# Two edits to a hand-made scheduler: due times without the delay inside an engine, and transfers planned to land later

## The chip, the cores and the metric

The kernel runs on 1 core of one Trainium2 chip. The metric is device time in microseconds from the first to the last work of one execution. Inputs and weights start in the chip's memory, all in float32, and the output goes back there.

## The reference

One layer of a hybrid encoder on 256 tokens of width 2048, with 256 fixed memory tokens:

```python
x = x + 0.5 * swiglu(rms_norm(x, ffn1_norm), ffn1_w_up, ffn1_w_down)      # d_ff 5632
h = rms_norm(x, mix_norm)
q_a, f_a, i_a, g_a, x_b, gate_b, gates = split(h @ w_in)
y_a = rms_norm(hgrn2(q_a, f_a, i_a)) * silu(g_a)          # gated linear recurrence, 8 heads
y_b = rglru(causal_conv4(x_b)) * gelu(gate_b)             # linear scan over the tokens
g = sigmoid(gates + b_gate)
x = x + (g[0] * (y_a @ w_branch_a) + g[1] * (y_b @ w_branch_b)) @ w_out
x = x + cross_attention(rms_norm(x), rms_norm(mem))       # 4 heads, wq, wkv, wo
x = x + 0.5 * swiglu(rms_norm(x, ffn2_norm), ffn2_w_up, ffn2_w_down)
return rms_norm(x, final_norm)
```

All weights together are several hundred MB and are read once.

## The kernel before

**The arithmetic.** Every large product is made of float32 parts that TensorE takes in one pass (`float32r`). A weight tile of 128 x 2048 (1 MB) is loaded into `raw`; ScalarE (ACT) writes its rounded high part `h`, VectorE (DVE) the rest `l = raw - h` (function `split`). The activations are split likewise. A product is then h·high + h·low + l·high, so each weight tile costs one ScalarE pass, one VectorE pass and three sets of matmuls.

**The stages.** In order: `ffn1`, the input projection ("in", "v", "gate") with the two recurrent branches in between, "ab" and "out", cross-attention ("q", "k", "mv", "o"), and `ffn2`. Three forms of product matter:

- `product` (stages "in", "q", "k"; 72 weight tiles): one bank of PSUM (the accumulators; there are eight) collects 16 matmuls of 512 columns with `h` as the stationary operand, and 16 of 256 columns with `l`. In the trace they are `acc<-ops,h` and `acc<-ops,l`.
- `rows_product` (stages "v", "gate", "ab", "out", "mv", "o"): two banks, the weights are the moving operand, all matmuls have 512 columns. In the trace `acc<-h,ops` and `acc<-l,ops`.
- `ffn`: the up projection combines two by two blocks with seven products instead of eight ("fast"); that needs sums of weight blocks (`td`, split into `th` and `tl`). Each of 11 blocks of hidden features ends with a chain on VectorE and ScalarE over the tile `ev`, transposes on TensorE, and the split operand `hidop`. The down projection ("down", 12 matmuls into each of two banks per weight tile) follows a few pieces later.

Two further ways to make a weight's parts: "added" (in `ffn1`) loads `own` on SP's queue, ScalarE writes `l = -round(own)`, and a DMA on POOL's queue adds `own` to it while it lands. "made" (for `ffn2`) computes block sums ahead of time, in the stages between the feed-forwards, and keeps them in the chip's memory: `made` is loaded, VectorE takes differences, and `kept` is stored by POOL's queue, to be read as `td` later.

**The order.** Nothing runs as it is written. `Flow.record` keeps each operation with the operations it depends on; `arrange` then plays the program through with modelled costs and writes one fixed sequence for all engines, which `emit` issues. The engines keep that sequence in hardware, each in its own order, waiting for each other on semaphores. What the planner uses:

- `price`: the modelled duration `op.busy` of each operation, and for a DMA the time `op.moved` that its bytes take in a shared pipe (2.9 us per MB, 5.2 us if it accumulates).
- `nominal`: the time at which a TensorE operation would start if TensorE ran the program as written without a hole.
- `aims`: from the last operation back, each operation's due time `op.due`. TensorE's operations start from their `nominal`; every operation is then due early enough for each of its successors, that is at `s.due - lag`. Successors include the next user of a buffer.
- `LAG`: per engine, the delay from the end of an operation to the start of its reader. `op.spent` is `op.busy` plus this delay, plus, for a DMA, `moved + LANDS`.
- In the play, each engine takes the ready operation with the lowest due time among those whose `nominal` is not more than `AHEAD` past the point reached. TensorE's true float32 operations (transposes and small products, marked `turn`) are gathered: within `STICK` of the first one due they may go ahead. A DMA waits while the pipe is filled for more than `BACKLOG`, its end is `dma + LANDS`, and the 9 to 13 big buffers are handed out by due time (`Ring.fit`).
- Between two operations of one engine the play already counts no `LAG` (it has `r = t + busy`, with 0.1 more on VectorE and ScalarE where the second reads the first's output); `aims` does.

The sequence is computed twice; the second time the due times follow the first sequence and its use of buffers.

Of the kernel before, what the change touches and what calls it, by code (L numbers as in the profile page):

```python
# [176 lines left out]


LAG = {"PE": 0.24, "DVE": 0.15, "ACT": 0.16, "POOL": 0.16, "SP": 0.1}
AHEAD, BACKLOG, STICK, LANDS = 30, 3, 8, 3.5  # L180
TABLES = {ACT.Silu, ACT.Sigmoid, ACT.Sqrt, ACT.Exp, ACT.Gelu_apprx_tanh}


class Flow:
# [97 lines left out]
    def aims(self, order):  # L282
        for op in self.ops:
            op.due = op.nominal if op.queue.name == "PE" or not op.after else 1e9
        for op in reversed(order):
            for s in op.after:
                lag = op.spent if s.deps.get(op, True) is not None else 0
                op.due = min(op.due, s.due - lag)

    def arrange(self):  # L290
# [1369 lines left out]
```

## Time and profile before

| | |
|---|---|
| median of 3 runs | 2427.21 us (2426.22 to 2428.08) |
| the profiled execution's own time | 2425.98 us |
| its span, first to last instruction | 2424.2 us |
| mean granted clock of TensorE | 0.999 |
| TensorE busy | 2408.9 us, 99% of the span, 12130 matmuls |
| VectorE busy | 2066.3 us, 85% |
| ScalarE busy | 1420.8 us, 59% |
| moved by DMA | 662.84 MB, mean 273 GB/s |

A profile is of one execution. "Busy" leaves out waiting, and the weight loads of TensorE (PEld) overlap its matmuls. Nearly all rows carry line 464, the one place where recorded operations are issued, so groups are told apart by their tiles: `acc<-ops,h` means that the bank `acc` was written from operand tiles `ops` and `h`. A duration of a matmul includes its way through the array: the distance between two starts, not the duration, is what one costs in a row of them.

### The profile page before, as it was taken

Reading aid. Unit: us, or ns where it says so; the run is one execution under the profiler, and the core shown is the slowest. Engines: PE = TensorE matmul, PEld = TensorE weight load, DVE = VectorE, ACT = ScalarE, POOL = GpSimd, SP = SyncE. Lnnn points to the kernel's source line nnn. Section 1 sums busy time; section 2 is a strip of 40 time slices with the busy share of each in tenths; the row PEclk is TensorE's granted clock in tenths of the full one; section 3 lists DMA queues with packets and bytes.
Section 4 is the critical chain, followed back from the end, with each engine's and each line's share of the span. In section 5 each row is a group of like instructions: output and inputs, shape, how many; then the busy total and the mean of one; then the engine's idle time right before and its main releaser. Section 6 shows DMA issues by size and latency. Waiting matters only on the chain. (4 is left out here: it accounts for less than half of the span.)

```text
span 2424.2 us, 30937 instructions
## 1 busy us (share of the span) xinstructions
PE 2408.9 (99%) x12130; PEld 2008.3 (83%) x12130; DVE 2066.3 (85%) x2232; ACT 1420.8 (59%) x1411; POOL 83.0 (3%) x142
## 2 busy tenths in 40 slices
PE   9999999999999999999999999999999999999998
PEld 8888888888888888888888888888888788888887
DVE  8999999999955778788876877867899999999995
ACT  8566666666654444467434644445676666666663
POOL 0000000000000000000000000000000000000000
PEclk9999999999999999999999999999999999999999
DMA  8568877877835677888989888886898777777773
GB/s 316 191 226 260 260 255 249 254 248 253 283 125 194 245 289 288 331 304 314 360 293 335 337 320 309 317 293 246 328 383 322 257 256 259 261 259 259 260 285 113
DMA packets 98355, 662.84 MB, mean 273 GB/s; under 512 B 10912, under 2 KB 11168, under 8 KB 24992
## 3 DMA queue, kind: packets, MB, share of 16 engines
q1 hardware_dynamic: 77904, 517.11, 57.5%
q0 software_dynamic: 19584, 142.62, 18.2%
q8 instruction: 95, 1.56, 0.2%
q10 hardware_dynamic: 720, 1.13, 0.1%
q14 instruction: 52, 0.43, 0.0%
HBM read 574.83 MB, written 60.82 MB: 262 GB/s over the span
## 5 line engine op out<-in xcount | busy, mean ns | idle before, releaser
L464 DVE TENSOR_TENSOR l<-raw,h 128x2048 fp32r<-128x2048 f32 (+2 forms) x428 | 870.9, 2039 | 163.6 <-PE acc L464 65.4
L464 ACT ACTIVATE h<-raw 128x2048 fp32r<-128x2048 f32 (+2 forms) x428 | 730.7, 1713 | 449.0 <-DVE l L464 182.0
L464 PE MATMUL acc<-h,xh 128*128 128x512 f32 x1244 | 471.1, 390 | 0.8 <-ACT h L464 0.3
L464 PE MATMUL acc<-h,xl 128*128 128x512 f32 x1244 | 449.3, 389 | 0.0
L464 PE MATMUL acc<-h,hidop 128*128 128x512 f32 x1408 | 440.0, 390 | 0.0
L464 ACT ACTIVATE h<-td 128x1024 fp32r<-128x1024 f32 (+1 forms) x248 | 308.1, 1251 | 199.7 <-DVE td L464 180.8
L464 PE MATMUL acc<-h,ops 128*128 128x512 f32 x1664 | 411.8, 391 | 0.0
L464 PE MATMUL acc<-ops,h 128*128 128x512 f32 x1152 | 391.8, 397 | 0.1
L464 DVE TENSOR_TENSOR tl<-td,h 128x1024 fp32r<-128x1024 f32 (+1 forms) x248 | 360.8, 1463 | 2.4 <-ACT h L464 0.7
L464 PEld LDWEIGHTS acc<-h,ops 128*128 128x128 f32 x1664 | 310.1, 188 | 63.7
L464 PEld LDWEIGHTS acc<-h,hidop 128*128 128x128 f32 x1408 | 262.9, 188 | 53.5
L464 PEld LDWEIGHTS acc<-h,xh 128*128 128x128 f32 x1244 | 233.1, 188 | 51.4 <-ACT h L464 2.0
L464 PEld LDWEIGHTS acc<-h,xl 128*128 128x128 f32 x1244 | 233.5, 188 | 48.3
L464 PE MATMUL acc<-ops,l 128*128 128x256 f32 x1152 | 273.5, 281 | 0.0
L464 PE MATMUL acc<-l,hidop 128*128 128x512 f32 x704 | 264.3, 390 | 2.0 <-DMA l<-own 1.9
L464 PEld LDWEIGHTS acc<-ops,h 128*128 128x128 f32 x1152 | 202.4, 188 | 32.9 <-DVE ops L464 0.9
L464 PEld LDWEIGHTS acc<-ops,l 128*128 128x128 f32 x1152 | 212.6, 188 | 19.8
L464 PE MATMUL acc<-l,ops 128*128 128x512 f32 x832 | 223.0, 390 | 0.0
L464 PE MATMUL acc<-tl,xh 128*128 128x512 f32 x608 | 187.6, 390 | 0.0
L464 PE MATMUL acc<-l,xh 128*128 128x512 f32 x636 | 186.2, 390 | 0.2 <-DVE l L464 0.2
L464 PEld LDWEIGHTS acc<-l,ops 128*128 128x128 f32 x832 | 155.5, 188 | 32.4 <-DVE l L464 0.4
L464 DVE TENSOR_TENSOR made<-made 128x512 f32<-128x512 f32 x224 | 153.4, 688 | 20.3 <-DMA made<-wu 16.7
(172 smaller groups left out, 1918.1 us busy)
## 6 DMA issues: line engine op xcount, KB each, us to landing
raw<-wu SPq DMA_DIRECT2D x108, 1024.0 KB, 7.7
raw<-wd SPq DMA_DIRECT2D x72, 1024.0 KB, 7.5
made<-wu POOLq DMA_DIRECT2D x56, 1024.0 KB, 6.5
kept<-made POOLq DMA_DIRECT2D x56, 1024.0 KB, 6.8
td<-kept SPq DMA_DIRECT2D x56, 1024.0 KB, 6.8
raw<-wu SPq DMA_DIRECT2D x56, 768.0 KB, 5.4
raw<-win SPq DMA_DIRECT2D x40, 1024.0 KB, 5.1
raw<-wg SPq DMA_DIRECT2D x32, 1024.0 KB, 6.5
```

What stands on the lines that cost most here:

```text
L464: getattr(op.queue.real, method)(*map(real, args), **{k: real(v) for k, v in kw.items()})
```

## The change

Two edits in the planner, none in the recorded operations.

In `aims`, the step from an operation to its successor is now the modelled duration alone where both are on the same engine and the first is no DMA; in all other cases with a dependence of order or data it is `op.spent` as before, and 0 where only the hand-out of the buffer is meant.

`LANDS`, the time after a transfer's turn in the pipe at which it is taken to have landed, goes from 3.5 to 4. It enters `op.spent`, so the due times, and the end of each transfer in the play.

```diff
-AHEAD, BACKLOG, STICK, LANDS = 30, 3, 8, 3.5
+AHEAD, BACKLOG, STICK, LANDS = 30, 3, 8, 4
...
             for s in op.after:
-                lag = op.spent if s.deps.get(op, True) is not None else 0
+                behind = s.queue is op.queue and not op.moved
+                lag = 0 if s.deps.get(op, True) is None else op.busy if behind else op.spent
                 op.due = min(op.due, s.due - lag)
```

## The prediction

> **What bounds the kernel now.** I read the page first, then busy time by stretches, TensorE's waits, and last the order of TensorE's matmuls in the stages that the two edits touch.
>
> ```profile
> span 2424.2 us, 30937 instructions
> PE 2408.9 (99%) x12130; PEld 2008.3 (83%) x12130; DVE 2066.3 (85%) x2232; ACT 1420.8 (59%) x1411; POOL 83.0 (3%) x142
> ```
>
> TensorE is busy for 2408.9 of 2424.2 us. 15.3 us are idle, so a better order can win little by filling holes, and a worse one has no upper bound. The profiled execution took 2425.98 us, 1.8 us more than its span and 1.23 us under the median of the runs, 2427.21. I make the sum as a difference and apply it to the median. About 0.2%, 4.85 us, is what a measurement of this kernel can tell from no change.
>
> Busy time by stretches, PE first and VectorE (DVE) third:
>
> ```profile
> 300.00:600.00 300.00, 297.95 (x1330) 245.68 (x1329) 280.87 (x287) 203.47 (x165) 13.01 (x15) 1.00 0.79 248
> 1500.00:1646.00 146.00, 144.93 (x720) 121.69 (x718) 106.09 (x139) 71.38 (x91) 9.62 (x18) 1.00 0.85 305
> 1900.00:2100.00 200.00, 199.76 (x892) 164.89 (x891) 197.90 (x171) 126.22 (x97) 0.00 (x0) 1.00 0.72 262
> 2300.00:2424.00 124.00, 115.22 (x517) 95.28 (x515) 92.78 (x88) 62.98 (x63) 0.00 (x0) 0.98 0.54 200
> ```
>
> 8.8 of the 15.3 us lie in the last stretch, mostly the closing norm and store after the last matmul. 2.05 us lie in 300 to 600, 1.07 in 1500 to 1646. In both feed-forward blocks VectorE is nearly full too: 280.87 of 300 and 197.90 of 200 us. TensorE's own waits:
>
> ```profile
> PE acc L464 <- DMA l<-own: 1.9, 3, 1.0
> PE acc L464 <- DVE p L464: 1.1, 2, 0.6
> PE warm L464 <- DVE ones L464: 1.1, 1, 1.1
> PE acc L464 <- DVE merge L464: 0.5, 1, 0.5
> PE acc L464 <- DVE sum L464: 0.4, 1, 0.4
> PE acc L464 <- ACT h L464: 0.3, 1, 0.3
> ```
>
> The largest is a transfer: the accumulating DMA that makes the low part `l` from `own` in the first feed-forward. The granted clock is 1.00 in all stretches but the last, so it plays no part.
>
> **The change, first edit: dues without the delay.** No instruction is added or removed; only `due`, the key by which the planner picks, moves. Of two operations of one engine the first was due the second's due minus its duration *and* the engine's `LAG`. Now it is the duration alone. TensorE's matmuls into one bank depend on each other, so each link of such a chain brought the earlier one forward by 0.24 us. In `product` (the column products of "in", "q" and "k") 32 matmuls in a row share a bank: 16 with `h` (512 columns), 16 with `l` (256). The first was due 31 x 0.24 = 7.4 us before its place in the program, the last at its place. As a product lasts some 5.6 us, the next product's `h` matmuls sort between the present one's `l` matmuls. The timeline shows just this mixing at its end, and then the last product alone; below it a row product, which has no long chain:
>
> ```profile
> 1535.46 0.40 PE L464 MATMUL acc<-ops,h 128*128 128x512 f32 x1
> 1535.69 0.28 PE L464 MATMUL acc<-ops,l 128*128 128x256 f32 x1
> 1535.81 0.39 PE L464 MATMUL acc<-ops,h 128*128 128x512 f32 x1
> ...
> 1536.50 2.08 PE L464 MATMUL acc<-ops,l 128*128 128x256 f32 x16
> 1538.42 0.40 PE L464 MATMUL acc<-h,ops 128*128 128x512 f32 x1
> ...
> 991.54 3.79 PE L464 MATMUL acc<-h,ops 128*128 128x512 f32 x16
> 995.17 1.98 PE L464 MATMUL acc<-l,ops 128*128 128x512 f32 x8
> ```
>
> Without the 0.24 every link's due equals its program place, and TensorE runs 16 `h`, then 16 `l`, product after product. That matters for the spacing. Alone, 16 `l` matmuls take from 1536.50 to 1538.42, 0.120 us each; 16 matmuls of 512 columns in a row take 991.54 to 995.17, 0.227 each. So a straight pair costs 0.347 us. Mixed, groups by form in two stretches with no other work (65 us, 1465 to 1530, then 60 us, 1380 to 1440) count:
>
> ```profile
> L464 PE MATMUL acc<-ops,h 128*128 128x512 f32 x185 | 61.9, 396 | 0.0
> L464 PE MATMUL acc<-ops,l 128*128 128x256 f32 x187 | 45.3, 281 | 0.0
> ...
> L464 PE MATMUL acc<-ops,h 128*128 128x512 f32 x172 | 57.5, 396 | 0.0
> L464 PE MATMUL acc<-ops,l 128*128 128x256 f32 x171 | 41.5, 281 | 0.0
> ```
>
> Straight, the first would take 185 x 0.227 + 187 x 0.120 = 64.4 of its 65 us, the second 59.6 of 60. That is 0.56 us saved on 185 pairs and 0.44 on 172. The page gives the whole count, and the same 6 ns in the means:
>
> ```profile
> L464 PE MATMUL acc<-h,ops 128*128 128x512 f32 x1664 | 411.8, 391 | 0.0
> L464 PE MATMUL acc<-ops,h 128*128 128x512 f32 x1152 | 391.8, 397 | 0.1
> ```
>
> 1152 pairs (72 products of 16, none missing) save 1152/185 x 0.56 = 3.5 or 1152/172 x 0.44 = 2.9 us; I take **-3.3 us**. TensorE is the path there, so it comes through whole. The ends: 0, if 0.233 belongs to these operands and not to the mixing; -6.9, if each mixed `h` loses 6 ns and the short `l` ones give nothing back.
>
> [...]
>
> In `down`, 12 matmuls share a bank and `h` ran up to 11 x 0.24 = 2.6 us early. All have 512 columns there, so straight order changes no spacing. It asks for `h` 2.6 us later, which loosens the loads. At the very end, token half 0's last matmul now has 12 behind it; before, 11:
>
> ```profile
> 2412.34 0.39 PE L464 MATMUL acc<-l,hidop 128*128 128x512 f32 x1
> 2412.56 1.75 PE L464 MATMUL acc<-h,hidop 128*128 128x512 f32 x7
> 2414.15 1.07 PE L464 MATMUL acc<-l,hidop 128*128 128x512 f32 x4
> ```
>
> So half 0's closing chain starts one matmul, **0.2 us**, earlier, and half 1's residual add, which comes after it on VectorE, has that much less ahead of it. Bounds: 0, if half 1's last matmul alone sets the end, and 0.23.
>
> VectorE's chains (sums of banks, `td`, `made`) become due 0.15 us later per link. They fall behind splits more often; the cover is the four pieces of 21 matmuls between a block's sums and its transposes, 4 x 21 x 0.227 = 19 us. I cost that at 0; its loss is the third rival.
>
> **The second edit: LANDS 4.** A 1 MB load is planned to land 2.9 + 0.06 + 4 = 6.96 us after its issue instead of 6.46; one that accumulates, 5.2 + 0.9 + 4 = 10.1 instead of 9.6. Each DMA on SP's and POOL's queues becomes due 0.5 us earlier, `own` and its accumulation together 1.0, and its readers are placed 0.5 us later. The trace's landings:
>
> ```profile
> raw<-wu SPq DMA_DIRECT2D x108, 1024.0 KB, 7.7
> td<-kept SPq DMA_DIRECT2D x56, 1024.0 KB, 6.8
> raw<-win SPq DMA_DIRECT2D x40, 1024.0 KB, 5.1
> l<-own POOLq DMA_DIRECT2D x24, 1024.0 KB, 8.8
> ...
> DMA to landing us min/median/max: 4.9/9.0/12.2
> ```
>
> The last line is the answer for `own`. The median of `wu` is above both planned values and `win`'s below both; the late tail (12.2) is what TensorE waits for. Half a microsecond to 1.0 covers most of three waits of at most 1.0: **-1.5 us** of the 1.9. Ends: -1.9, and +22 if all 24 accumulations came to wait the longest 1.0; three did, so I stay near that row. A buffer held 0.5 us longer is hidden by columns taken later and costs 0.
>
> By the Trainium skill, "DMA: Bandwidth & Descriptors", where its two cost components stand, a transfer takes about 2.0 us + bytes / 436 GB/s, an estimated 4.4 us for 1 MB; then 3.5 was already too late, the edit goes the wrong way, and the sum would be -3.5. Every median above is higher, so the trace speaks for the larger value.
>
> Sum: -3.3 - 0.2 - 1.5 = -5.0, so 2427.21 - 5.0 = **2422.2 us**; the case's own range, with its bounds, is 2419 to 2425.
>
> **The rivals.** *Spacing is not the order's.* 0.233 us then stays; what remains is -1.7, 2425.5. For it: `h` is the stationary operand only in these products. Against: no other term than the short neighbour explains it, and the row product with the same tile sizes has 0.227. Chance 0.12.
>
> *All waits go.* Columns asked for 7.4 us later leave every load ready, and the five waits for data among the rows above, 1.9 + 1.1 + 0.5 + 0.4 + 0.3 = 4.2 us, disappear: -3.3 - 0.2 - 4.2, 2419.5. Against: `p`, `merge` and `sum` (2.0 us) are the latency of one chain at a stage's end. Chance 0.09.
>
> *VectorE's chains come late (slower).* In the feed-forwards VectorE has 2.1 us free in 200. A block's sums, due less early, go behind a 2.04 us split, the transposes miss their 19 us, and TensorE waits once a block, as it does here for a split (start to start 0.81 us instead of 0.23):
>
> ```profile
> 1889.35 0.48 PE L464 MATMUL acc<-h,xl 128*128 128x512 f32 x1
> 1890.16 0.72 PE L464 MATMUL acc<-h,xh 128*128 128x512 f32 x2 [0.33 <-ACT h L464]
> L464 DVE TENSOR_TENSOR l<-raw,h 128x2048 fp32r<-128x2048 f32 (+2 forms) x428 | 870.9, 2039 | 163.6 <-PE acc L464 65.4
> ```
>
> 22 blocks x 0.58 = 12.8, less 5.0: +7.8, 2435.0. It decides from 9 blocks on, where 9 x 0.58 = 5.2 cancels the gain. For it: no spare VectorE time. Against: a 19 us cover for 5 links x 0.15 us. Chance 0.16.
>
> *The order hardly changes*: other reasons than the chain set the dues; 2427.2. Chance 0.03.
>
> **How the numbers follow.** The forecast has 0.60; 0.34 of it beyond the 0.2% bound at 2422.4, 0.26 within. Faster 0.34 + 0.09 = 0.43; same 0.26 + 0.12 + 0.03 = 0.41; slower 0.16. The range 2417.5 to 2431 takes in the forecast with both bounds, the first, second and fourth rival, and the near end of the third; it leaves out the rest of that, some 0.12, and little below.
>
> **What would show it.** Right: runs of 16 `ops,h` then 16 `ops,l` in the timeline, `ops,h` at a mean near 391, the waits for `l<-own` under 0.5 us, the last stretch 0.2 us shorter. Wrong: mixing as before; unmixed columns with mean 397; new waits of TensorE for `hidop`, `ev`, `h` or `l` from VectorE after 1780 us, or for `raw` and `own` loads.

## The result and the profile after

The changed kernel takes 2415.88 us (median of 5 runs, 2414.86 to 2417.24) against 2427.21: a ratio of 0.9953, 95% interval 0.9938 to 0.9967. It is 11.3 us faster where 5.0 were forecast, and it lies below the range of 2417.5 to 2431. The direction was right, the size was not.

The profiled execution, the page's head:

```profile
span 2414.1 us, 30928 instructions
PE 2402.7 (100%) x12130; PEld 2011.3 (83%) x12130; DVE 2066.0 (86%) x2232; ACT 1421.3 (59%) x1414; POOL 83.2 (3%) x142
```

The span fell by 10.1 us, TensorE's busy time by 6.2, with the same 12130 matmuls. So part of the gain lies inside what the page calls busy. TensorE's waits now, and the column products' groups:

```profile
PE warm L465 <- DVE ones L465: 1.1, 1, 1.1
PE acc L465 <- ACT h L465: 0.9, 1, 0.9
PE acc L465 <- DVE gate L465: 0.6, 1, 0.6
PE acc L465 <- DVE x L465: 0.3, 1, 0.3
PE acc L465 <- DVE ops L465: 0.2, 1, 0.2
...
L465 PE MATMUL acc<-ops,h 128*128 128x512 f32 x1152 | 278.3, 393 | 0.3 <-DVE ops L465 0.2
L465 PE MATMUL acc<-ops,l 128*128 128x256 f32 x1152 | 150.0, 283 | 0.0
```

The waits for `l<-own`, `p`, `merge` and `sum` are gone (the wait for `gate` is new, the one for `h` longer), and `ops,h` fell from a mean of 397 ns to 393. The timeline of TensorE shows the straight order that the prediction named, 16 and 16:

```profile
1418.02 2.08 PE L465 MATMUL acc<-ops,l 128*128 128x256 f32 x16
1419.93 3.82 PE L465 MATMUL acc<-ops,h 128*128 128x512 f32 x16
1423.59 2.08 PE L465 MATMUL acc<-ops,l 128*128 128x256 f32 x16
1425.50 1.78 PE L465 MATMUL acc<-ops,h 128*128 128x512 f32 x7
```

One product takes 1423.59 - 1418.02 = 5.57 us. Three stretches of busy time, to be read beside those of before:

```profile
300.00:600.00 300.00, 300.00 (x1345) 248.40 (x1344) 283.31 (x290) 205.22 (x167) 13.03 (x15) 1.00 0.79 254
1500.00:1646.00 146.00, 146.00 (x726) 123.53 (x725) 108.59 (x153) 75.59 (x108) 8.57 (x16) 1.00 0.75 279
1900.00:2100.00 200.00, 200.00 (x894) 165.31 (x893) 197.28 (x167) 125.66 (x96) 0.00 (x0) 1.00 0.73 268
```

The first two have no idle TensorE time left (2.05 and 1.07 us before). For a full account I took the starts of TensorE's matmuls from both traces and subtracted from each distance the steady one (0.227 us after a 512-column matmul, 0.120 after a 256-column one, and the medians of the small float32 kinds). What is left over, in us, summed by part of the program:

| part | before | after | difference |
|---|---|---|---|
| spacing in the column products, without waits | 4.0 | 1.1 | -2.9 |
| first feed-forward, where `l<-own` waited | 4.7 | 0.9 | -3.8 |
| attention scores and values | 3.1 | 0.8 | -2.3 |
| after the last matmul's start | 9.35 | 8.58 | -0.8 |
| all else | | | -0.3 |
| span | 2424.2 | 2414.1 | -10.1 |

Each column is one execution; the five executions of the changed kernel differ among themselves by up to 2.4 us.

### The profile page after: what moved, and what is told of

It reads as the page before. It is cut to its first block, busy times and chain, and to the rows that moved or that the text cites. A ratio compares the mean times of both kernels' runs of the same rounds, so it can differ in the third digit from the quotient of the medians.

```text
span 2414.1 us, 30928 instructions
## 1 busy us (share of the span) xinstructions
PE 2402.7 (100%) x12130; PEld 2011.3 (83%) x12130; DVE 2066.0 (86%) x2232; ACT 1421.3 (59%) x1414; POOL 83.2 (3%) x142
## 4 chain that ended last, share of the span: by engine, by line
PE 98%; ACT 1%; DVE 1%; DMA 1%; issue 0%; ACTq 0%; DVEq 0%
PE acc L465 98%; DMA made<-wu 1%; ACT h L465 0%; PE warm L465 0%; DVE l L465 0%; ACT ops L465 0%; DVE made L465 0%; DVE ops L465 0%; ACT junk L465 0%; ACT x L465 0%; DVE ss L465 0%; DVE x L465 0%; DVE gate L465 0%; DVE xc L465 0%; ACTq L465 0%
## 5 line engine op out<-in xcount | busy, mean ns | idle before, releaser
L465 PE MATMUL acc<-h,xh 128*128 128x512 f32 x1244 | 484.5, 390 | 0.9 <-ACT h L465 0.9
L465 PE MATMUL acc<-h,xl 128*128 128x512 f32 x1244 | 484.0, 389 | 0.0
L465 PE MATMUL acc<-h,ops 128*128 128x512 f32 x1664 | 398.0, 391 | 0.6 <-DVE gate L465 0.6
L465 PE MATMUL acc<-h,hidop 128*128 128x512 f32 x1408 | 355.2, 390 | 0.0
L465 PE MATMUL acc<-ops,h 128*128 128x512 f32 x1152 | 278.3, 393 | 0.3 <-DVE ops L465 0.2
L465 PE MATMUL acc<-l,ops 128*128 128x512 f32 x832 | 206.2, 389 | 0.0
L465 PE MATMUL acc<-l,hidop 128*128 128x512 f32 x704 | 190.3, 389 | 0.0
L465 PE MATMUL acc<-tl,xh 128*128 128x512 f32 x608 | 168.2, 390 | 0.0
L465 PEld LDWEIGHTS acc<-l,hidop 128*128 128x128 f32 x704 | 132.2, 188 | 27.5
L465 PEld LDWEIGHTS acc<-ops,l 128*128 128x128 f32 x1152 | 148.0, 191 | 5.6
```

What stands on the lines that cost most here:

```text
L465: getattr(op.queue.real, method)(*map(real, args), **{k: real(v) for k, v in kw.items()})
```

## The experiments

In all of them the ratio is to the kernel before, run on the same chip in the same rounds; spans are of the profiled executions. The profiled execution of the kernel before (2425.98 us) lies 1.2 to 3.0 us under that kernel's medians in the several rounds (2427.21 to 2428.93), so differences between spans come out smaller than differences between medians.

### One edit at a time

**e1_lag**: the first edit alone.

```diff
-AHEAD, BACKLOG, STICK, LANDS = 30, 3, 8, 4
+AHEAD, BACKLOG, STICK, LANDS = 30, 3, 8, 3.5
```

> The first edit alone, LANDS stays at 3.5. Theory L (the landing time cures the waits for l<-own): columns run straight, ops,h at a mean near 393 ns and some 3 us saved there, the waits of TensorE for l<-own stay near 2 us, in all about 4 to 6 us under the kernel before. Theory O (the order of TensorE alone does it): the waits for l<-own go without the later landing too, in all 9 to 11 us under the kernel before.

Measured: 2415.53 us, ratio 0.9944 (0.9932 to 0.9957), span 2413.3. No wait for `l<-own`, `ops,h` at 393 ns. The first edit alone gives the whole gain; beside the changed kernel's 2415.88 the second adds nothing that these intervals could tell.

**e2_lands**: the second edit alone (the kernel before with LANDS 4).

> The second edit alone, dues as before. Theory L: columns stay mixed (ops,h mean 397 ns), the waits for l<-own fall below 0.5 us, in all 3 to 5 us under the kernel before. Theory O: waits for l<-own stay, within 1.5 us of the kernel before.

Measured: 2421.20 us, ratio 0.9971 (0.9960 to 0.9983), span 2418.9. `ops,h` stays at 397, the waits for `l<-own` go. So each edit cures that wait without the other. Neither theory L, which had it stay in e1_lag, nor theory O, which had it stay here, holds.

**e3_lag_pe** and **e4_lag_others**: the first edit for TensorE's chains alone, and for all but TensorE's, both with LANDS 3.5.

```diff
-                behind = s.queue is op.queue and not op.moved
+                behind = s.queue is op.queue and not op.moved and op.queue.name == "PE"
```

(e4_lag_others has `!=` in place of `==`.)

> The first edit for TensorE's own chains alone, the other engines' dues as before, LANDS 3.5. Both theories: straight columns, ops,h near 393 ns, some 3 us saved there. Theory O: the same time as the first edit whole, within 1.5 us. A third theory V (VectorE's and ScalarE's chains matter at the ends of stages, where TensorE waited for p, merge and sum for 2.0 us): those waits stay here, and the time is 2 to 3 us above the first edit whole.

> The first edit for all engines but TensorE, LANDS 3.5. Columns stay mixed, ops,h at 397 ns. Theory O: within 1.5 us of the kernel before. Theory V: the waits for p, merge and sum shrink, 2 to 3 us under the kernel before. If VectorE's chains come late in the feed-forwards, as the third rival has it, new waits for hidop or h after 1740 us and a time above the kernel before.

Measured: e3_lag_pe 2415.56 us, ratio 0.9949 (0.9935 to 0.9963), span 2412.7; e4_lag_others 2421.25 us, ratio 0.9967 (0.9955 to 0.9980), span 2418.6. TensorE's dues carry the gain whole, and the waits for `p`, `merge` and `sum` go with them, so theory V falls. Yet the other engines' dues alone give 5.6 us of span, with mixed columns, and there, too, the waits for `merge` and `sum` go. Where from? TensorE's longest waits in e4_lag_others:

```profile
PE warm L465 <- DVE ones L465: 1.1, 1, 1.1
PE acc L465 <- DVE p L465: 0.8, 1, 0.8
PE acc L465 <- DVE l L465: 0.4, 2, 0.2
PE acc L465 <- ACT h L465: 0.3, 1, 0.3
```

Again no `l<-own`. Four different changes of the dues all removed the waits for this one kind of transfer. That asks what was special about it.

### The wait for own

ScalarE's timeline around the longest of these waits, before, with the issue of the DMA and TensorE's matmul:

```profile
320.59 1.92 ACT L464 ACTIVATE h<-raw 128x2048 fp32r<-128x2048 f32 x1 [0.32 <-PE acc L464]
324.91 0.72 ACT L464 ACTIVATE ev<-ev,rtok 128x512 f32<-128x512 f32 x1 [2.40 <-DVE ev L464]
325.54 1.90 ACT L464 ACTIVATE l<-own 128x2048 fp32r<-128x2048 f32 x1
...
327.84 0.87 POOL L464 DMA_DIRECT2D l<-own  x1 [20.36 <-DVE l L464]
...
340.09 0.50 PE L464 MATMUL acc<-l,hidop 128*128 128x512 f32 x1 [0.97 <-DMA l<-own]
340.43 0.39 PE L464 MATMUL acc<-h,hidop 128*128 128x512 f32 x1
...
DMA to landing us min/median/max: 6.3/9.0/12.2
```

The block chain's SiLU on `ev` stands ahead of the rounding `l<-own`, waits 2.40 us for VectorE, and the rounding waits behind it. The accumulating DMA is issued only after the rounding, at 327.84, lands 12.2 us later (the last line is for the DMAs of `own` in 300 to 345 us), and TensorE's matmul follows at 340.09. Eight of the 24 roundings stand behind an `ev` operation in this way, one in each block that uses them. After the change none does; the same place:

```profile
319.96 1.90 ACT L465 ACTIVATE l<-own 128x2048 fp32r<-128x2048 f32 x1
321.77 1.90 ACT L465 ACTIVATE h<-own 128x2048 fp32r<-128x2048 f32 x1
323.57 1.90 ACT L465 ACTIVATE h<-raw 128x2048 fp32r<-128x2048 f32 x1
325.37 0.71 ACT L465 ACTIVATE ev<-ev,rtok 128x512 f32<-128x512 f32 x1
...
322.27 0.87 POOL L465 DMA_DIRECT2D l<-own  x1 [17.75 <-ACT l L465]
...
DMA to landing us min/median/max: 4.8/7.2/12.0
```

The DMA goes out at 322.27, 5.6 us earlier. It is again the slowest of the stretch and takes 12.0 us, yet TensorE does not wait for it: the late issue, not a slower landing, set the wait. Two more runs tested this.

**e5_own_first**: the kernel before; only the due time of the rounding is 0.5 us earlier, in all 24 places where it occurs.

```diff
-        act.activation(l, raw, ACT.Copy, scale=-1.0)
+        act.activation(l, raw, ACT.Copy, scale=-1.0).early = 0.5
...
                 op.due = min(op.due, s.due - lag)
+            op.due -= op.early
```

> The kernel before with one thing changed: the rounding l<-own on ScalarE is due 0.5 us earlier, so that it goes ahead of the block chain's ev<-ev,rtok where the two are close. Theory Q (the waits for l<-own came from that one place in ScalarE's queue, where the rounding stood behind an ev operation that itself waited 2.4 us for VectorE): the four waits in 300 to 600 us go, some 3.4 us under the kernel before, columns stay mixed. Theory P (the accumulation lands late because the DMA pipe is full): the waits stay, within 1 us of the kernel before.

Measured: 2423.05 us, ratio 0.9985 (0.9976 to 0.9994), span 2421.2, 3.0 under before. ScalarE's timeline at that place, and TensorE's longest wait:

```profile
318.94 1.91 ACT L465 ACTIVATE l<-own 128x2048 fp32r<-128x2048 f32 x1
320.75 1.90 ACT L465 ACTIVATE h<-own 128x2048 fp32r<-128x2048 f32 x1
322.55 1.90 ACT L465 ACTIVATE h<-raw 128x2048 fp32r<-128x2048 f32 x1
325.36 0.72 ACT L465 ACTIVATE ev<-ev,rtok 128x512 f32<-128x512 f32 x1 [0.91 <-DVE ev L465]
...
PE acc L465 <- DVE p L465: 2.0, 1, 2.0
```

The order turned and TensorE no longer waits for `l<-own`: what was left over in that stretch fell by 3.4 us, as theory Q has it. The wait for `p`, more than a thousand microseconds later, where nothing was edited, rose from 1.1 to 2.0 and took some of it back.

**e9_lands36**: the kernel before with LANDS 3.6.

> The kernel before with LANDS 3.6, a fifth of the second edit. Theory N (the waits for l<-own are a near tie of two due times on ScalarE, and any nudge turns it): the waits go, 3 to 4 us under the kernel before. Theory P (the landing needs the whole 0.5 us): the waits shrink by a fifth at most, within 1.5 us of the kernel before. Columns stay mixed in both.

Measured: 2421.94 us, ratio 0.9978 (0.9969 to 0.9987), span 2419.5. TensorE's two longest waits:

```profile
PE warm L464 <- DVE ones L464: 1.1, 1, 1.1
PE acc L464 <- ACT h L464: 0.7, 2, 0.4
```

A fifth of the second edit removes the waits for `l<-own`; the rounding goes ahead of the `ev` operation there too, and what was left over in that stretch fell by 3.4 us. So theory N holds for these waits: in the second edit, it was not half a microsecond of landing time that helped but the turn of a near tie, that is, of two operations of one engine whose due times are almost the same. That any nudge turns it does not hold: in e7_columns and e10_scores below the waits stay.

The run gained more than theory N has, 4.7 us of span, largely because the waits for `p`, `merge` and `sum` went as well, though the due times of the score matmuls follow the same rule as in the kernel before. In the attention stretch some 2.2 us less was left over. These waits, too, hang on small shifts of the due times.

### The columns

**e6_alternate**: the changed kernel, `h` and `l` alternating inside each product.

```diff
-        high(range(KT - 4))
-        was_late = bool(late)
-        if was_late:
+        if late:
+            high(range(KT - 4))
             flush(late)
             low(range(KT - 4))
-        high(range(KT - 4, KT))
-        low(range(KT - 4 if was_late else 0, KT))
+            high(range(KT - 4, KT))
+            low(range(KT - 4, KT))
+            return acc
+        for k in range(KT):
+            high([k])
+            low([k])
```

(The product that has late work to flush is left as it was.)

> The changed kernel with the program order inside a column product altered: h and l matmuls alternate (h0, l0, h1, l1 and so on) in place of 16 h and then 16 l; one product still follows the other. Theory S (a 512-column matmul with a 256-column neighbour takes 0.233 us in place of 0.227 to 0.228, a 256-column one 0.118 in place of 0.120): ops,h back to a mean near 397 ns and 3 to 4 us above the changed kernel, that is 8 to 9 us under the kernel before. Theory T (the gain in the columns came from finishing product after product, not from the neighbours): ops,h stays near 393 ns and the time within 1 us of the changed kernel.

Measured: 2418.79 us, ratio 0.9964 (0.9952 to 0.9977), 2.9 us over the changed kernel by the medians. The profiled execution took 2422.02 us, 3.2 over the median; its span is 2420.2, 6.1 over the changed kernel's. The groups and the timeline:

```profile
L465 PE MATMUL acc<-ops,h 128*128 128x512 f32 x1152 | 405.0, 399 | 1.0 <-DVE ops L465 1.0
L465 PE MATMUL acc<-ops,l 128*128 128x256 f32 x1152 | 318.5, 281 | 0.9 <-DVE l L465 0.8
...
1419.61 0.39 PE L465 MATMUL acc<-ops,h 128*128 128x512 f32 x1
1419.84 0.27 PE L465 MATMUL acc<-ops,l 128*128 128x256 f32 x1
1419.96 0.40 PE L465 MATMUL acc<-ops,h 128*128 128x512 f32 x1
1420.19 0.28 PE L465 MATMUL acc<-ops,l 128*128 128x256 f32 x1
```

Product still follows product, yet `ops,h` is at 399 ns. The distance from an `h` to the next start, waits left out, is 0.2347 us on average here, 0.2327 in the kernel before, 0.2285 in the changed one; after an `l` it is 0.1168, 0.1179 and 0.1195. Of the 6.1 us in the one execution, 3.9 are this spacing, in line with theory S; the rest is mostly waits, of which the two groups show 1.9 (that they come from `l` being needed half a product earlier was not tested). So the neighbour sets the spacing, not the finishing order.

**e7_columns**, **e8_ffn**, **e10_scores**: the kernel before, the first edit only between matmuls of one kind: column products, feed-forwards, attention scores.

```diff
-                lag = op.spent if s.deps.get(op, True) is not None else 0
+                lag = 0 if s.deps.get(op, True) is None else op.busy if op.chain and s.chain else op.spent
```

with `chain` set on those matmuls where they are recorded.

> The kernel before with the first edit for the matmuls of the column products alone. Expected by the terms of the prediction: straight columns, ops,h near 393 ns, 2.9 to 3.4 us under the kernel before, the waits for l<-own and the closing stretch as before. If the order of the columns also decides the waits for p and sum after 1540 us, up to 2.3 us more.

> The kernel before with the first edit for the matmuls of the feed-forwards alone (up and down). Expected: columns mixed as before, ops,h 397 ns; straight order in the down products moves the dues around l<-own, so its waits go (3.4 us), and token half 0 closes 24 matmuls before the end (0.8 us less after the last matmul): about 4 us under the kernel before. If l<-own still waits, under 1.5 us.

> The kernel before with the first edit for the attention score matmuls alone (8 in a row into one bank). Theory C (these matmuls, due up to 1.7 us early in pieces, let the softmax chain of p end late): the waits for p and sum in 1540 to 1650 us go, 1.5 to 2.2 us under the kernel before; l<-own, columns and the close as before. Theory D (they go only because the columns ahead are straight): within 0.7 us of the kernel before.

| | median | ratio, interval | span | against before's |
|---|---|---|---|---|
| e7_columns | 2422.27 | 0.9977 (0.9968 to 0.9985) | 2420.5 | -3.7 |
| e8_ffn | 2420.77 | 0.9973 (0.9962 to 0.9983) | 2419.3 | -4.9 |
| e10_scores | 2424.75 | 0.9988 (0.9979 to 0.9997) | 2423.7 | -0.5 |

e7_columns has the spacing (2.9 us) and keeps the waits for `l<-own`. e8_ffn loses them (what was left over in the first feed-forward fell by 3.5 us) and closes 0.8 us sooner. By the medians the three are 5.2, 6.7 and 3.0 us under the kernel before. e10_scores, by theory C, empties the attention stretch (what was left over there fell from 3.1 to 0.7 us); but the waits of TensorE in e10_scores are these:

```profile
PE acc L465 <- DMA l<-own: 4.2, 7, 1.4
PE warm L465 <- DVE ones L465: 1.1, 1, 1.1
PE acc L465 <- ACT h L465: 0.3, 1, 0.3
```

An edit to matmuls at 1540 us made the waits for `l<-own` in the first feed-forward worse, from 3 to 7. Due times are worked out from the last operation back, so a later stage can move an earlier one; by which path it did so here was not followed. The three parts together, -3.7, -4.9 and the 2.4 us of the attention stretch, of which e7_columns had 0.8 already, come to -10.2 beside e3_lag_pe's -11.5.

### The other way, and a try for more

**e11_lag_lands3**: the first edit with LANDS 3. **e12_lag_stick14**: the first edit with LANDS 3.5 and STICK 14.

> The first edit with LANDS 3, the other way. If the landing time matters by itself: TensorE waits for loads, 3 us and more above the changed kernel. If it only shifts ties: within 2 us of the changed kernel and of the first edit alone, no wait for a DMA.

> A try for a faster version: the first edit with LANDS 3.5 and STICK 14, so that TensorE's true float32 operations wait for each other longer and it changes over less often (each change costs some 0.11 us at the first matmul after it). If fewer changes are left: 1 to 2 us under the first edit alone. If gathering makes transposes late: new waits of ScalarE and VectorE, and the same time or more.

Measured: e11_lag_lands3 2420.85 us, ratio 0.9974 (0.9964 to 0.9985), span 2418.7. A load is now late; its waits and TensorE's timeline:

```profile
PE acc L465 <- DMA lw<-lruw: 2.1, 1, 2.1
PE acc L465 <- DVE p L465: 1.8, 1, 1.8
...
1110.44 5.38 PE L465 MATMUL acc<-xc,lw 128*128 128x256 f32 x16 [2.11 <-DMA lw<-lruw]
```

It is issued at 1100.1 us and lands 10.2 us later; with LANDS 3.5 the same load was issued at 1097.1. The issue moved by 3.0 us, six times as much as LANDS, and the wait for `p` is back as well, so this run does not show whether the plan's landing was too short or the order of the loads turned. Between 3.5 and 4, under the first edit, LANDS shows no effect. e12_lag_stick14: 2417.33 us, ratio 0.9961 (0.9948 to 0.9973), span 2413.4, no better than the first edit alone. TensorE went over to its true float32 operations 75 times in it and 77 times in e1_lag, so hardly a change was saved. No version that beats the changed kernel was found.

## Why the prediction missed

**The columns: right in mechanism, nearly in size.** -3.3 was forecast; the spacing gave 2.9. The `h` of a straight product costs 0.2285 us, a little over the 0.227 taken from the row products. The Trainium skill, "TensorE: Matmul & The Clock Gate", section "Back-to-back issue gap", gives the gap of an isolated warm matmul by its column count alone, N / 2.4 + 2.5 ns; in the stream of e6_alternate the neighbour counts too, 0.2347 against 0.2285 us for the same matmul.

**The second edit's term: wrong in cause and in size.** The step that failed is "Half a microsecond to 1.0 covers most of three waits", -1.5 us.

- The cause: TensorE did wait for a transfer that landed 12.2 us after its issue, as the prediction read. But after the change the same transfer took 12.0 us and TensorE did not wait, because it was issued 5.6 us earlier. ScalarE's queue had held it up (e5_own_first). Either of the two edits turned that order, so what was credited to LANDS belongs to either alone, and with the first edit made the second adds nothing that the runs could tell.
- The size: it was read from the wait view, 1.9 us. That view counts only the time past a matmul's modelled end. A matmul lasts 0.39 us and the next normally starts 0.227 after it, so every hole is shown some 0.16 us too small, and after each of these waits the next matmul came 0.34 us later (340.09 to 340.43), 0.11 more than the steady distance. Distances between starts give 3.8 us for the stretch. The wait view of the weight loads (PEld) in the kernel before already named six waits, of 4.3 us in all, where that of the matmuls showed three:

```profile
PEld acc L464 <- DMA l<-own: 4.3, 6, 1.4
```

The rule weighed there, from the Trainium skill's "DMA: Bandwidth & Descriptors", the two cost components, gives an estimated 4.4 us for 1 MB. The medians in this trace, 5.1 to 8.8 us, do not agree with it. Planning by it would mean an earlier landing; e11_lag_lands3 went half a microsecond that way, and its span was 5.4 us over the first edit's with 3.5, for a cause that stays open.

**The waits of the attention stretch: costed at 0.** The second rival had them go, but I held `p` and `sum` for latency that no order could hide. In fact the order could: with the score matmuls straight the softmax chain ends in time (e10_scores), and with LANDS 3.6 it does so with the score matmuls mixed as before (e9_lands36). So straight score matmuls are enough, but not needed. This cost the forecast 2.3 us.

**The close: 0.2 forecast, 0.8 measured.** The bound of 0.23 was wrong. I counted 12 matmuls behind token half 0's last one in place of 11; the straight order put half 0's last matmul a whole further group of 12 ahead, as the timeline of the close shows:

```profile
2399.37 1.07 PE L465 MATMUL acc<-l,hidop 128*128 128x512 f32 x4
2400.28 1.98 PE L465 MATMUL acc<-h,hidop 128*128 128x512 f32 x8
2400.48 0.69 DVE L465 SCALAR_TENSOR_TENSOR x<-acc,x 128x512 f32<-128x512 f32 x1 [3.04 <-PE acc L465]
...
2405.92 0.69 DVE L465 SCALAR_TENSOR_TENSOR x<-acc,x 128x512 f32<-128x512 f32 x1 [2.09 <-PE acc L465]
```

Half 0 is added at 2400.48, 24 matmuls ahead of the end, its close is off VectorE when half 1 is due, and half 1's add runs at once. e8_ffn, the first edit between matmuls of the feed-forwards alone, has the same 0.8 us.

**The third rival did not come.** VectorE's 197.28 of 200 us left TensorE without a hole in that stretch, and e4_lag_others, which is that rival's edit alone, is faster. **The range** ended too high because its lowest case took the wait view's 4.2 us as all there was to win.

**The sum.** Forecast beside measured, in spans: columns -3.3 and -2.9, `l<-own` -1.5 and -3.8, attention 0 and -2.3, the close -0.2 and -0.8, all else 0 and -0.3; together -5.0 and -10.1. The medians differ by 1.2 us more, by which the profiled execution before lay under its median. The columns were foreseen. That the two kinds of waits went was luck as far as the prediction goes: e10_scores, a part of the first edit, made the waits for `l<-own` longer, and e5_own_first the wait for `p`.

Open: why exactly the softmax chain is late in the kernel before was not followed further than e10_scores and e9_lands36. The 0.3 us of "all else" is a balance, some 0.9 us less in the second feed-forward and 0.6 more elsewhere, and its causes were not followed.

## What to carry to other kernels

In a list-scheduled kernel that is full on one engine, size the possible gain from distances between starts on that engine, stretch by stretch, not from its listed waits. When a change of priorities removes a wait, look in each engine's queue for an operation that stood waiting ahead of the one that mattered, and try a nudge a fifth as large: if that removes it too, the wait was a near tie. Such ties turn in stages that nobody edited, by about one to three microseconds in these runs, so compare the stage that you edited and not the total alone. Where the order is free, keep matmuls of unequal width in runs rather than alternating; here that was worth 2.9 us.

## What the runs showed of the hardware

A 512-column matmul took 0.2347 us to the next start when it alternated with 256-column ones, 0.2285 in runs of 16; the 256-column ones gave back less (0.1168 against 0.1195). After each of the three waits of TensorE for `l<-own` in the kernel before, the matmul that resumed was followed 0.34 us later, not 0.227. The prediction had the first of these in its sum, the second not.
